# Natural projections 512 columns wide over all token tiles at once, and TensorE's large tiles at multiples of 256 bytes

## The chip, the cores and the metric

The kernel runs on one core of a Trainium2 chip. The metric is the device time of one execution in microseconds; three runs of the kernel before took 2058.98, 2060.18 and 2060.73 us, median 2060.18 us. Five engines work in a core: TensorE (PE in the profile) multiplies, VectorE (DVE), ScalarE (ACT) and GpSimd (POOL) do the rest, and SyncE (SP) issues the DMAs. TensorE accumulates in PSUM, which has eight banks of 512 floats in each of 128 partitions; the other engines read the results there.

## The reference

One layer of a hybrid decoder trunk over a prompt of 2048 tokens and a sample group of 8 x 8 = 64 tokens, model width 1024, all in float32. Cut to what matters here:

```
h = rmsnorm(x) @ w_in                                   # 1024 columns in, all branches out
q, k, v, z_a, gate_b, gate_c, h_b, z_b, u, v_c, z_c, g = split(h)
q = rmsnorm(q per head of 64); k = rmsnorm(k per head)   # q: 512 columns, 8 heads
y_a = window attention(q, k, v)                          # banded, 128 positions, sinks
y_b = gate_b * causal_conv3(gate_c * h_b)
v_c = rmsnorm(v_c)                                       # 512 columns, one norm per token
y_c = u * (tril(w_s[group]) @ v_c + b_s)                 # mixing of the 128 positions of a chunk
m = sum over branches of sigmoid(g_i) * ((silu(z_i) * y_i) @ w_out_i)
y = x + m @ w_o
```

The change touches how q and v_c (the chunk v) are projected and normed, and where tiles lie in memory. What is computed stays the same.

## The kernel before

**Precision.** Every float32 operand of a large product is split (`split`, L167 on ScalarE and L168 on VectorE) into a high part that TensorE takes at full rate and a low rest; each product is three matmuls: high x high, high x low, low x high.

**Two forms of product.** In the *transposed* form (`gemm_t`, L176 to L178) a 128x128 weight block is stationary and the tokens move, 512 columns at a time: `xh`, `xl` (the split normed input), `mh`, `ml` (the merged branches) or `br0h` to `br2l` (the branch outputs). In the *natural* form (`natural`, L285 to L287) 128 tokens are stationary and 256 weight columns move, so that a token's features lie along the free dimension and can be normed there. A natural token tile is 8 blocks of 128 rows x 3 matmuls = 24 matmuls.

**Stages.** The tokens go through in four superblocks of four token tiles; the last also has the 64 sample tokens, and its 576 columns move as two chunks of 288. In each superblock: `kv_phase` (natural), `q_phase` (natural, two passes of 256 columns over all token tiles, each tile evicted from its own `ps_mm` buffer, of which there are three), z_A and the convolution branch (transposed, with attention between them), `chunk_phase` (u and z_C transposed, then v natural), `gate_phase` (per 128 output columns and branch 24 matmuls with `xh`/`xl`, then 12 with `br`), `out_phase` (`m`). The chunk v goes through in two passes: the first puts 256 columns of all four token tiles into the four quarters of the PSUM tile `first`, the second puts the other 256 columns of a tile into a `ps_mm`, after which that tile is evicted.

**Evictions.** Of q: ScalarE squares (L297), VectorE sums per head (L299), POOL forms the inverse root (`rstd`, L163 and L164), VectorE multiplies (L390). Of chunk v: ScalarE squares and sums each half (L688), VectorE adds the halves (L692), POOL (L163, L164), VectorE multiplies each half (L697), `split` into `vbuf`; 2.5 and 3.0 ticks later two `spatial` pieces mix the tile's positions: four matmuls each into a `ps_tp` (two buffers; L674, L675), two additions on VectorE (L677, L678), after the second a multiply (L653) and a split into `br2`.

**What sets the order.** Each engine runs its instructions in the order of the program. Weights arrive as units of 512 KB (256 KB for w_out), loaded by SP and split ahead of use in a fixed list (`order`, `take`). Pieces of other work are put between the matmuls by `later(delay, fn)`; `tick` advances a clock by 0.25 for every six matmuls of 512 columns (every twelve of a natural tile of 256), and runs what is due. Tiles of one `tag` share memory; the framework makes an instruction wait where it would overwrite what another engine has still to read, and it tracks this by PSUM tile.

**Addresses.** Tiles are laid out per partition in the order of their allocation. `consts` comes first, then `xh`, `xl`, `kst`, `vst` and `hist` (32 bytes) in `res`, then the rest. In the program as built, `xh`, `xl`, `kst`, `vst` and `wsp` start 32 bytes above a multiple of 256, and what lies behind `hist` (`mh`, `ml`, `br*`, `rbuf`, `vbuf`, the weights `wh`, `wl`) 64 bytes above one.

Of the kernel before, what the change touches and what calls it, by code (L numbers as in the profile page):

```python
# [20 lines left out]
NTS = NS * TS  # L21
NT = SEQ + NTS
HD = 64
EPS = 1e-6
KT = D // P
# [23 lines left out]
def trunk_kernel(ctx: ExitStack, tc: tile.TileContext, A, O):  # L49
    nc = tc.nc  # L50
# [8 lines left out]
    def ps_mm():  # L59
        return psum.tile([P, 512], F32, tag="mm", name="ps_mm", bufs=3)  # L60
# [93 lines left out]
    xh = res.tile([P, KT, TMAX], F32R, name="xh")  # L154
    xl = res.tile([P, KT, TMAX], F32R, name="xl")
    kst = res.tile([P, 2, 5, P], F32R, name="kst")
    vst = res.tile([P, 5 * 256 + 128], F32R, name="vst")
    hist = res.tile([P, 4, 2], F32, name="hist")
    nc.vector.memset(hist, 0.0)

    def rstd(out, ssq, n, width):

        nc.gpsimd.tensor_scalar(out, ssq, 1.0 / width, EPS, ALU.mult, ALU.add)  # L163
        nc.gpsimd.tensor_tensor(out, out, mhalf[: out.shape[0], :n], ALU.pow)  # L164
# [127 lines left out]
    def nunits(chunk):  # L292
        return [take("wn", 2 * chunk + j) for j in range(2)]

    def head_rstd(src, rows, nh, tag):
        sq = side("sq", [P, nh * HD])
        nc.scalar.activation(sq[:rows], src, AF.Square)  # L297
        s = small.tile([P, nh], F32, tag=tag + "s", name=tag + "s")
        nc.vector.tensor_reduce(s[:rows], sq[:rows].rearrange("p (h d) -> p h d", d=HD), AX.X, ALU.add)  # L299
# [75 lines left out]
    def q_phase(sb, samp):  # L375
        _, ntile, _, sample = SBS[sb]
        qn = res.tile([P, 4 * TMAX], F32, tag="br2l", name="qn")
        abuf = samp["abuf"]
        samp["q"] = [x[:NTS, 2048:2304] for x in (qn, abuf)]
        for g in range(2):  # L380
            w = nunits(1 + g)
            for i in range(ntile + sample):
                rows = NTS if i == ntile else P
                o = natural(ps_mm()[:rows, :256], i, rows, w)
                r = head_rstd(o, rows, 4, "q")
                if i == ntile:
                    dst = samp["q"][g]
                else:
                    dst = qn[:, i * 512 + g * 256: i * 512 + (g + 1) * 256]
                nc.vector.scalar_tensor_tensor(  # L390
                    dst.rearrange("p (h d) -> p h d", d=HD),
                    o.rearrange("p (h d) -> p h d", d=HD),
                    HD ** -0.5,
                    r[:rows].unsqueeze(2).broadcast_to([rows, 4, HD]),
                    ALU.mult,
                    ALU.mult,
                )
        return qn, abuf
# [100 lines left out]
    def sample_attention(samp, sbuf, za, br):  # L499
# [24 lines left out]
        def scores(g):  # L524
            kts = samp["kts"]
            sp = psum.tile([P, 2, 256], F32, tag="S", name="sps", bufs=1)
            gs = slice(g * HD, (g + 1) * HD)
            for n in range(NS):
                nn, j = divmod(n, 4)
                lhs = qts[gs, n * 32:(n + 1) * 32]  # L530
                rs = slice(32 * j, 32 * j + 32)
                nc.tensor.matmul(sp[rs, nn, 0:P], lhs, kc[gs, n * P:(n + 1) * P], start=True, stop=True)
                nc.tensor.matmul(sp[rs, nn, P:w], lhs, kts[gs], start=True, stop=True)
            s = sbuf[:, g * 1024:g * 1024 + 2 * w].rearrange("p (a b) -> p a b", a=2)
            nc.sync.dma_start(s, A["biass"][:, g])
            nc.vector.tensor_tensor(s, sp[:, :, 0:w], s, ALU.add)
            nm = small.tile([P, 2], F32, tag="snm", name="snm")
            nc.vector.tensor_reduce(nm, s, AX.X, ALU.max, negate=True)
            nc.vector.tensor_tensor(nm, nm, nsinks_s[:, g:g + 1].broadcast_to([P, 2]), ALU.min)
            den = small.tile([P, 2], F32, tag="sden", name="sden")  # L540
            for nn in range(2):
                nc.scalar.activation(s[:, nn], s[:, nn], AF.Exp, bias=nm[:, nn:nn + 1], accum_out=den[:, nn:nn + 1])
            es = small.tile([P, 2], F32, tag="ses", name="ses")
# [80 lines left out]
    def chunk_phase(sb, br, samp_args):  # L624
# [17 lines left out]
        if sample:  # L642
            os.append(psum.tile([P, 512], F32, tag="pv", name="sfirst", bufs=1)[:NTS, :256])
        w = nunits(3)
        for i in range(ntile + sample):
            natural(os[i], i, NTS if i == ntile else P, w)
        w = nunits(4)

        def mixed(i, rows, t, gg):

            ts = slice(i * P, i * P + rows)
# [27 lines left out]
            if gg.stop == 4:  # L679
                mixed(i, P, t, slice(0, 4))  # L680

        for i in range(ntile + sample):
            rows = NTS if i == ntile else P
            o2 = [os[i][:rows], natural(ps_mm()[:rows, :256], i, rows, w)]
            ssq = small.tile([P, 2], F32, tag="vssq", name="vssq")
            vn = tmp("vn", [P, 512])
            for j in range(2):
                nc.scalar.activation(  # L688
                    vn[:rows, j * 256:(j + 1) * 256], o2[j], AF.Square, accum_out=ssq[:rows, j:j + 1]
                )  # L690
            s1 = small.tile([P, 1], F32, tag="vs1", name="vs1")
            nc.vector.tensor_tensor(s1[:rows], ssq[:rows, 0:1], ssq[:rows, 1:2], ALU.add)  # L692
            r = small.tile([P, 1], F32, tag="vr", name="vr")
            rstd(r[:rows], s1[:rows], 1, 512)
            for j in range(2):
                js = slice(j * 256, (j + 1) * 256)
                nc.vector.scalar_tensor_tensor(vn[:rows, js], o2[j], r[:rows], vnw[:rows, js], ALU.mult, ALU.mult)  # L697
# [157 lines left out]
def _layout(i):  # L855
# [20 lines left out]
    for d in range(KT):  # L876
        order += [tl["g"][8 * b + d] for b in range(3)]
    a["wt"] = np.stack(order)
    nat = [np.concatenate([c["k"], c["v"]], 1), c["q"][:, :256], c["q"][:, 256:], c["vc"][:, :256], c["vc"][:, 256:]]

    a["wn"] = np.stack([x.reshape(2, 4, P, 256).transpose(0, 2, 1, 3) for x in nat]).reshape(10, P, 1024)
# [74 lines left out]
```

## Time and profile before

| | |
|---|---|
| median of three runs | 2060.18 us |
| the profiled execution, its own time | 2059.51 us |
| its span, first to last instruction | 2057.7 us |
| TensorE busy | 2037.0 us, 99 % |
| VectorE, ScalarE, POOL busy | 51 %, 41 %, 5 % |
| mean granted TensorE clock | 0.997 |
| matmul groups L176 to L178 | 749.7 + 740.4 + 740.5 us for `xh`/`xl`, 112.5 + 112.6 + 112.6 us for `m` |
| natural groups L285 to L287 into `ps_mm` | 156.4 + 154.1 + 154.3 us |

The profile is of one execution; 1.8 us of its time lie outside its span. A group's row has busy time, mean duration of one in ns, and the idle time ahead of them with what ended it. A timeline row has start, duration, engine, line, operation, tile written and tiles read. A matmul's duration holds its pipeline, so neighbours overlap; how fast they follow each other is read from their starts.

### The profile page before, as it was taken

How to read it: one execution, taken by the hardware profiler on the slowest of the kernel's cores; microseconds unless marked ns; L12 is line 12 of the kernel's file. 1: busy time of each engine (PE TensorE's matmuls, PEld its weight loads, DVE VectorE, ACT ScalarE, POOL GpSimd, SP SyncE). 2: the span in 40 equal slices, each digit the busy share in tenths (PEclk: the TensorE clock that was granted, in tenths of full speed). 3: DMA queues.
4: the chain of work that ended last, by engine and by line, in shares of the span. 5: the costliest groups of instructions: out<-in, count | busy, mean ns of one | idle time of the engine just before them, and what ended most of it. 6: DMA issues, size and time to landing. Idle time of an engine off the chain costs nothing.

```text
span 2057.7 us, 29142 instructions
## 1 busy us (share of the span) xinstructions
PE 2037.0 (99%) x11703; PEld 1794.7 (87%) x11703; DVE 1057.5 (51%) x1869; ACT 850.8 (41%) x1513; POOL 96.2 (5%) x168
## 2 busy tenths in 40 slices
PE   6999999999999999999999999999999999999999
PEld 6888888888988898888988888888899999999999
DVE  6586253335588353335478535334557842533332
ACT  5675233332576233333367423333347641422330
POOL 3100000000200000000200000000030000000000
PEclk9999999999999999999999999999999999999999
DMA  6222233336222223335322223333622341222233
GB/s 192 94 82 82 82 102 119 117 108 220 83 77 78 93 74 116 113 95 192 129 93 70 84 72 106 125 105 120 201 87 52 56 129 57 65 83 88 78 103 107
DMA packets 85702, 212.36 MB, mean 103 GB/s; under 512 B 18224, under 2 KB 23344, under 8 KB 85552
## 3 DMA queue, kind: packets, MB, share of 16 engines
q1 hardware_dynamic: 85536, 209.53, 32.7%
q8 instruction: 92, 1.51, 0.3%
q10 hardware_dynamic: 32, 0.98, 0.1%
q14 instruction: 42, 0.34, 0.1%
HBM read 201.46 MB, written 10.00 MB: 103 GB/s over the span
## 4 chain that ended last, share of the span: by engine, by line
PE 98%; ACT 1%; DVE 1%; DMA 0%; POOL 0%; issue 0%; SPq 0%; DVEq 0%
PE ps_mm L176 27%; PE ps_mm L177 27%; PE ps_mm L178 27%; PE ps_mm L287 3%; PE ps_mm L285 3%; PE ps_mm L286 3%; PE ps_tp L468 1%; PE sp L444 1%; PE sp L443 1%; PE first L287 1%; PE first L286 1%; PE first L285 1%; PE pv L475 1%; PE pv L476 1%; PE ps_tp L674 0%; PE ps_tp L675 0%
## 5 line engine op out<-in xcount | busy, mean ns | idle before, releaser
L176 PE MATMUL ps_mm<-xh,wh 128*128 128x512 f32 (+1 forms) x2080 | 749.7, 360 | 0.5 <-ACT za L830 0.5
L178 PE MATMUL ps_mm<-xh,wl 128*128 128x512 f32 (+1 forms) x2080 | 740.5, 356 | 0.0
L177 PE MATMUL ps_mm<-xl,wh 128*128 128x512 f32 (+1 forms) x2080 | 740.4, 356 | 0.0
L168 DVE TENSOR_TENSOR wl<-raw,wh 128x1024 fp32r<-128x1024 f32 x376 | 407.4, 1085 | 528.4 <-ACT wh L167 526.2
L167 ACT CAST wh<-raw 128x1024 fp32r<-128x1024 f32 x376 | 353.0, 940 | 722.4 <-PE ps_mm L177 554.6
L178 PEld LDWEIGHTS ps_mm<-xh,wl 128*128 128x128 f32 x2080 | 392.6, 189 | 56.2
L176 PEld LDWEIGHTS ps_mm<-xh,wh 128*128 128x128 f32 x2080 | 392.6, 189 | 52.5 <-ACT za L830 0.7
L177 PEld LDWEIGHTS ps_mm<-xl,wh 128*128 128x128 f32 x2080 | 393.2, 189 | 51.1
L285 PE MATMUL ps_mm<-wh,xh 128*128 128x256 f32 (+1 forms) x544 | 156.4, 287 | 5.0 <-ACT xh L167 5.0
L286 PE MATMUL ps_mm<-wl,xh 128*128 128x256 f32 (+1 forms) x544 | 154.1, 283 | 1.3 <-DVE wl L168 1.3
L287 PE MATMUL ps_mm<-wh,xl 128*128 128x256 f32 (+1 forms) x544 | 154.3, 284 | 0.9 <-DVE xl L168 0.9
L177 PE MATMUL ps_mm<-ml,wh 128*128 128x512 f32 (+1 forms) x320 | 112.6, 352 | 0.3 <-DVE ml L168 0.3
L178 PE MATMUL ps_mm<-mh,wl 128*128 128x512 f32 (+1 forms) x320 | 112.6, 352 | 0.0
L176 PE MATMUL ps_mm<-mh,wh 128*128 128x512 f32 (+1 forms) x320 | 112.5, 351 | 0.0
L742 DVE TENSOR_TENSOR t<-ps_mm,t 128x512 f32<-128x512 f32 (+1 forms) x120 | 71.5, 596 | 76.6 <-PE ps_mm L178 75.2
L285 PEld LDWEIGHTS ps_mm<-wh,xh 128*128 128x128 f32 (+1 forms) x544 | 102.8, 189 | 6.5 <-ACT xh L167 6.3
L286 PEld LDWEIGHTS ps_mm<-wl,xh 128*128 128x128 f32 (+1 forms) x544 | 102.7, 189 | 1.8 <-DVE wl L168 1.6
L287 PEld LDWEIGHTS ps_mm<-wh,xl 128*128 128x128 f32 (+1 forms) x544 | 102.6, 189 | 1.4 <-DVE xl L168 1.3
L726 ACT ACTIVATE t<-ps_mm,c_bg 128x512 f32<-128x512 f32 (+1 forms) x120 | 73.0, 609 | 72.4 <-PE ps_mm L178 72.3
L431 ACT ACTIVATE rbuf<-ps_tp,c_qnw 64x256 fp32r<-64x256 f32 x128 | 60.0, 469 | 23.8 <-PE ps_tp L423 12.4
L177 PEld LDWEIGHTS ps_mm<-ml,wh 128*128 128x128 f32 x320 | 60.1, 188 | 7.9 <-DVE ml L168 0.6
L176 PEld LDWEIGHTS ps_mm<-mh,wh 128*128 128x128 f32 x320 | 60.1, 188 | 7.5
(203 smaller groups left out, 2565.2 us busy)
## 6 DMA issues: line engine op xcount, KB each, us to landing
raw<-in_wt SPq DMA_DIRECT2D x208, 512.0 KB
raw<-in_wout SPq DMA_DIRECT2D x96, 256.0 KB
raw<-in_wn SPq DMA_DIRECT2D x40, 512.0 KB
raw<-in_wo SPq DMA_DIRECT2D x32, 512.0 KB
xbuf<-in_xn SPq DMA_DIRECT2D x12, 512.0 KB
xt<-in_xt SPq DMA_DIRECT2D x24, 256.0 KB
out_yt<-xt SPq DMA_DIRECT2D x24, 256.0 KB
xbuf<-in_xt SPq DMA_DIRECT2D x16, 256.0 KB
```

What stands on the lines that cost most here:

```text
L167: nc.scalar.copy(hi, src)
L168: nc.vector.tensor_tensor(lo, src, hi.bitcast(F32), ALU.subtract)
L176: nc.tensor.matmul(o, wh[:, ws], rh(k, c0, c1), start=k == 0, stop=False)
L177: nc.tensor.matmul(o, wh[:, ws], rl(k, c0, c1), start=False, stop=False)
L178: nc.tensor.matmul(o, wl[:, ws], rh(k, c0, c1), start=False, stop=k == kts - 1)
L285: nc.tensor.matmul(o, xh[:, k, ts], wh[:, ws], start=k == 0, stop=False)
L286: nc.tensor.matmul(o, xh[:, k, ts], wl[:, ws], start=False, stop=False)
L287: nc.tensor.matmul(o, xl[:, k, ts], wh[:, ws], start=False, stop=k == KT - 1)
L431: nc.scalar.activation(hh[half, :, e], src, AF.Copy, scale=qnw2[es])
L443: nc.tensor.matmul(sp[:, h, k0:], b["hh"][:, hs], rhs, start=True, stop=False)
L726: nc.scalar.activation(t[:, c0:c1], pg[:, : c1 - c0], AF.Sigmoid, bias=bg[:, 8 * b + d:8 * b + d + 1])
L742: nc.vector.tensor_tensor(t[:, c0:c1], pa[:, : c1 - c0], t[:, c0:c1], ALU.mult)
```

## The change

Two edits.

1. `q_phase` and the chunk v use `wide`: the outer loop runs over four weight units of 2 blocks x 512 columns (the layout of the units in memory is changed for it), the inner one over the token tiles, six matmuls of 512 columns each. All accumulators of 512 columns are open at once: token tiles 0 and 1 in the halves of one PSUM tile `wide`, tile 2 in `widep`, tile 3 (and the sample) in `ps_mm`. A tile is evicted as soon as its six matmuls of the last unit are issued: q with one square, one sum over eight heads, one inverse root of eight, two multiplies; chunk v with one square, one inverse root, one multiply.
2. `hist` moves to `consts` and an unused tile of 192 bytes follows it. In the program as built, `xh`, `xl`, `kst`, `vst`, `wsp`, `mh`, `ml`, `br*`, `rbuf`, `vbuf`, `wh` and `wl` all start at a multiple of 256 bytes. Three small sample tiles (`snm`, `sden`, `ses`) get two buffers instead of four.

```diff
-    hist = res.tile([P, 4, 2], F32, name="hist")
+    hist = consts.tile([P, 4, 2], F32, name="hist")
+
+    consts.tile([P, 48], F32, name="pad")
...
+    def wide_outs(n, sample):
+
+        s4 = psum.tile([P, 4, 256], F32, tag="S", name="wide", bufs=1)
+        outs = [s4[:, 0:2].rearrange("p a b -> p (a b)"), s4[:, 2:4].rearrange("p a b -> p (a b)")]
+        outs.append(psum.tile([P, 512], F32, tag="pv", name="widep", bufs=1)[:, :])
+        outs += [ps_mm()[:, :] for _ in range(n + sample - 3)]
+        return [(o[:NTS] if i == n else o[:, :], NTS if i == n else P) for i, o in enumerate(outs)]
+
+    def wide(j0, outs):
+
+        for u in range(4):
+            wh, wl = take("wn", j0 + u)
+            for i, (o, rows) in enumerate(outs):
+                ts = slice(i * P, i * P + rows)
+                for kk in range(2):
+                    k = 2 * u + kk
+                    ws = slice(kk * 512, (kk + 1) * 512)
+                    nc.tensor.matmul(o, xh[:, k, ts], wh[:, ws], start=k == 0, stop=False)
+                    nc.tensor.matmul(o, xh[:, k, ts], wl[:, ws], start=False, stop=False)
+                    nc.tensor.matmul(o, xl[:, k, ts], wh[:, ws], start=False, stop=k == KT - 1)
+                tick(0.25)
+                if u == 3:
+                    yield i, o, rows
...
-        for g in range(2):
-            w = nunits(1 + g)
-            for i in range(ntile + sample):
-                rows = NTS if i == ntile else P
-                o = natural(ps_mm()[:rows, :256], i, rows, w)
-                r = head_rstd(o, rows, 4, "q")
...
+        for i, o, rows in wide(2, wide_outs(ntile, sample)):
+            r = head_rstd(o, rows, 8, "q")
+            for g in range(2):
+                gs = slice(g * 256, (g + 1) * 256)
+                dst = samp["q"][g] if i == ntile else qn[:, i * 512 + g * 256: i * 512 + (g + 1) * 256]
                 nc.vector.scalar_tensor_tensor(
                     dst.rearrange("p (h d) -> p h d", d=HD),
-                    o.rearrange("p (h d) -> p h d", d=HD),
+                    o[:, gs].rearrange("p (h d) -> p h d", d=HD),
                     HD ** -0.5,
-                    r[:rows].unsqueeze(2).broadcast_to([rows, 4, HD]),
+                    r[:rows, 4 * g:4 * g + 4].unsqueeze(2).broadcast_to([rows, 4, HD]),
...
-        first = psum.tile([P, 4, 256], F32, tag="S", name="first", bufs=1)
-        os = [first[:, i] for i in range(ntile)]
...
-        w = nunits(3)
-        for i in range(ntile + sample):
-            natural(os[i], i, NTS if i == ntile else P, w)
-        w = nunits(4)
...
-        for i in range(ntile + sample):
-            rows = NTS if i == ntile else P
-            o2 = [os[i][:rows], natural(ps_mm()[:rows, :256], i, rows, w)]
...
+        for i, o, rows in wide(6, wide_outs(ntile, sample)):
+            ssq = small.tile([P, 1], F32, tag="vssq", name="vssq")
             vn = tmp("vn", [P, 512])
...
+            nc.scalar.activation(vn[:rows], o, AF.Square, accum_out=ssq[:rows])
             r = small.tile([P, 1], F32, tag="vr", name="vr")
-            rstd(r[:rows], s1[:rows], 1, 512)
...
+            rstd(r[:rows], ssq[:rows], 1, 512)
+            nc.vector.scalar_tensor_tensor(vn[:rows], o, r[:rows], vnw[:rows], ALU.mult, ALU.mult)
```

The units keep their size, number and place in SP's list. On TensorE, 1632 natural matmuls of 256 columns become 816 of 512.

The first place is TensorE at the end of the first superblock's q. Before, the border between two token tiles of the second pass (a tile's last matmuls, then the next tile's first into another buffer):

```order
L285 MATMUL ps_mm<-wh,xh 128x256
L286 MATMUL ps_mm<-wl,xh 128x256
L287 MATMUL ps_mm<-wh,xl 128x256
L285 MATMUL ps_mm<-wh,xh 128x256 [waits DVE_49,Activation_49]
L286 MATMUL ps_mm<-wl,xh 128x256
```

After, the same place in the last unit: the end of tile 3's six matmuls of the unit before, tile 0's six, and the start of tile 1's:

```order
L316 MATMUL ps_mm<-wh,xl 128x512
L314 MATMUL wide<-wh,xh 128x512 [waits Activation_49]
L315 MATMUL wide<-wl,xh 128x512 [waits DVE_49]
L316 MATMUL wide<-wh,xl 128x512
L314 MATMUL wide<-wh,xh 128x512
L315 MATMUL wide<-wl,xh 128x512
L316 MATMUL wide<-wh,xl 128x512
L314 MATMUL wide<-wh,xh 128x512 [waits DVE_49,Activation_49]
L315 MATMUL wide<-wl,xh 128x512
```

Before, the wait on VectorE and ScalarE is for the reads of the tile that held this `ps_mm` buffer three tiles ago. After, the wait of tile 1's first matmul is for the reads of tile 0, whose six matmuls stand just ahead of it; tile 0's own two waits are for the split weights of the unit.

The second place is VectorE's queue there. Before, the last two evictions of q, of 256 columns each:

```order
L168 TENSOR_TENSOR wsp<-wsr,wsp 128x4x128 [waits Activation_49]
L299 TENSOR_REDUCE qs<-sq 128x4 [waits Activation_49]
L390 SCALAR_TENSOR_TENSOR qn<-ps_mm,qr 128x256 [waits Pool_49]
L168 TENSOR_TENSOR wl<-raw,wh 128x1024 [waits DMAHW3_49,Activation_49]
L299 TENSOR_REDUCE qs<-sq 128x4 [waits Activation_49]
L168 TENSOR_TENSOR wl<-raw,wh 128x1024 [waits DMAHW4_49,PE_49,Activation_49]
L390 SCALAR_TENSOR_TENSOR qn<-ps_mm,qr 128x256 [waits Pool_49]
```

After, all of tile 0's and tile 1's:

```order
L325 TENSOR_REDUCE qs<-sq 128x8 [waits Activation_49]
L170 TENSOR_TENSOR wsp<-wsr,wsp 128x4x128 [waits Activation_49]
L411 SCALAR_TENSOR_TENSOR qn<-wide,qr 128x256 [waits Pool_49]
L411 SCALAR_TENSOR_TENSOR qn<-wide,qr 128x256
L325 TENSOR_REDUCE qs<-sq 128x8 [waits Activation_49]
L411 SCALAR_TENSOR_TENSOR qn<-wide,qr 128x256 [waits Pool_49]
```

A tile's sum, its wait for POOL and its two multiplies now follow each other, and tile 1's sum stands behind tile 0's multiplies; `wsp` (split once, in the first superblock) stands inside.

The third place is TensorE at the start of `gate_phase` in the first superblock, where the spatial pieces come due. Before, two of them, then twelve `br0` matmuls, of which the first two are shown, ahead of the next four:

```order
L674 MATMUL ps_tp<-wsp,vbuf 128x256
L675 MATMUL ps_tp<-wsp,vbuf 128x256
L674 MATMUL ps_tp<-wsp,vbuf 128x256
L675 MATMUL ps_tp<-wsp,vbuf 128x256
L176 MATMUL ps_mm<-br0h,wh 128x512
L177 MATMUL ps_mm<-br0l,wh 128x512
```

After, between two such groups stand six:

```order
L686 MATMUL ps_tp<-wsp,vbuf 128x256
L687 MATMUL ps_tp<-wsp,vbuf 128x256
L178 MATMUL ps_mm<-xh,wh 128x512
L179 MATMUL ps_mm<-xl,wh 128x512
L180 MATMUL ps_mm<-xh,wl 128x512
L178 MATMUL ps_mm<-xh,wh 128x512
L179 MATMUL ps_mm<-xl,wh 128x512
L180 MATMUL ps_mm<-xh,wl 128x512
L686 MATMUL ps_tp<-wsp,vbuf 128x256
L687 MATMUL ps_tp<-wsp,vbuf 128x256
```

The groups of spatial matmuls stand six matmuls apart where they stood twelve apart.

More of the change, by code (lines that the diff above doesn't have):

```diff
@@ L639, in chunk_phase @@
         vbuf = res.tile([P, 4 * 1024], F32R, tag="mh", name="vbuf")
-        first = psum.tile([P, 4, 256], F32, tag="S", name="first", bufs=1)
-        os = [first[:, i] for i in range(ntile)]
-        if sample:
-            os.append(psum.tile([P, 512], F32, tag="pv", name="sfirst", bufs=1)[:NTS, :256])
-        w = nunits(3)
-        for i in range(ntile + sample):
-            natural(os[i], i, NTS if i == ntile else P, w)
-        w = nunits(4)
         def mixed(i, rows, t, gg):
@@ L878, in _layout @@
     a["wt"] = np.stack(order)
-    nat = [np.concatenate([c["k"], c["v"]], 1), c["q"][:, :256], c["q"][:, 256:], c["vc"][:, :256], c["vc"][:, 256:]]
-    a["wn"] = np.stack([x.reshape(2, 4, P, 256).transpose(0, 2, 1, 3) for x in nat]).reshape(10, P, 1024)
+    kv = np.concatenate([c["k"], c["v"]], 1).reshape(2, 4, P, 256)
+    a["wn"] = np.concatenate(
+        [kv.transpose(0, 2, 1, 3).reshape(2, P, 1024)]
+        + [x.reshape(4, 2, P, 512).transpose(0, 2, 1, 3).reshape(4, P, 1024) for x in (c["q"], c["vc"])]
+    )
     wa = np.asarray(i["w_out_a"])[0][perm]
```

20 lines of the change are left out of this document (3 added, 17 removed).

## The prediction

> **What bounds the kernel now.** I read the page first, then the waits of TensorE, then its time table, in that order: does TensorE ever stop, and how fast do its matmuls follow each other when it does not.
>
> ```profile
> span 2057.7 us, 29142 instructions
> PE 2037.0 (99%) x11703; PEld 1794.7 (87%) x11703; DVE 1057.5 (51%) x1869; ACT 850.8 (41%) x1513; POOL 96.2 (5%) x168
> PE 98%; ACT 1%; DVE 1%; DMA 0%; POOL 0%; issue 0%; SPq 0%; DVEq 0%
> PE ps_tp L266 <- POOL xr L164: 8.8, 3, 6.5
> PE ps_mm L285 <- ACT xh L167: 5.0, 4, 4.0
> ...
> PE ps_tp L674 <- DVE sp L678: 0.2, 1, 0.2
> ```
>
> TensorE is busy 99 % of the span, 98 % of the chain that ended last is its own, and its waits add up to under 20 us, nearly all before the first superblock's stream is running. So the time is the number of matmuls times their pitch (start to start), and two things can change it: the pitch, or a new stop. A matmul's listed duration holds its pipeline; the pitch comes from stretches without a gap (start, duration, PE busy, matmuls, granted clock, DMA share, GB/s; the count takes in one that reaches in from before):
>
> ```profile
> core 0: us, PE busy (x), PEclk, DMA share, GB/s
> 188.07:237.07 49.00, 49.00 (x211) 1.00 0.29 92
> 237.07:259.47 22.40, 22.40 (x193) 1.00 0.17 59
> 464.12:507.65 43.53, 43.53 (x193) 1.00 0.69 230
> 1656.37:1674.53 18.16, 18.16 (x138) 1.00 0.38 88
> 2015.90:2041.34 25.44, 25.44 (x194) 1.00 0.36 114
> ```
>
> The first row is z_C/u tiles with `xh`, `xl` moving, 512 columns: 49.00/210 = 233.3 ns. The second is the natural projection of v, 256 columns: 22.40/192 = 116.7 ns. The third is `mh`, `ml`, 512 columns: 43.53/192 = 226.7 ns, at a DMA share twice as high, so traffic is not what makes the first row slow. The last two are 288 columns, `xh`/`xl` 18.16/137 = 132.6, `mh`/`ml` 25.44/192 = 132.5. The program's addresses differ in one respect: `xh`, `xl` start 32 bytes above a multiple of 256, the `m`, `br` and weight tiles 64 bytes above one. The groups by shape say the same in modelled durations:
>
> ```profile
> L177 PE MATMUL ps_mm<-xl,wh 128*128 128x512 f32 x1248 | 493.9, 396 | 0.0
> L177 PE MATMUL ps_mm<-ml,wh 128*128 128x512 f32 x192 | 74.8, 389 | 0.0
> L177 PE MATMUL ps_mm<-br1l,wh 128*128 128x512 f32 x96 | 37.7, 392 | 0.0
> ```
>
> **The gain.** After the change all of these start at a multiple of 256, a start that no row shows. I take for it the best pitch that is shown, 226.7, and keep two bounds: no gain, and the removal of all that does not grow with columns. For the second: from 288 to 512 columns the pitch grows by (226.7 - 132.5)/224 = 0.42 ns a column, 215.3 ns for 512.
> - 512-column `xh`/`xl`: 3 x 1248 = 3744 matmuls x 6.6 = 24.7 us.
> - `br`: 9 groups of 96 = 864, whose groups stand 2 to 3 ns above `m` because they follow `xh`: 864 x 2 = 1.7 us.
> - q and chunk v: 17 token tiles x 24 x 2 products = 816 matmuls of 512 columns take the place of 1632 of 256. At the old start this is nothing, 2 x 116.7 = 233.4 against 233.3; at 226.7 it is 816 x 6.7 = 5.5 us.
> - 288 columns, kv (still 256) and attention: nothing, since the two 288 rows agree within 0.1 ns; the bound is in the first rival.
>
> Sum: **-32 us**. The Trainium skill (TensorE: Matmul & The Clock Gate, "Back-to-back issue gap") states N/2.4 GHz plus about 2.5 ns between warm matmuls, 215.8 ns for 512 columns. No row here is that fast; by it 512-column matmuls lose another 10.9 ns each.
>
> **The new stop.** Before, a token tile's 24 matmuls were finished one tile after another, each into its own `ps_mm` (or a quarter of `first`, which was full before anything read it). Now all four finish in the last weight unit, six matmuls apart, and token tiles 0 and 1 are halves of one PSUM tile, `wide`. As the order shows, tile 1's first matmul of that unit waits for the engines that evict tile 0; TensorE issues in order, so tiles 2 and 3 queue behind it. This happens for q and for chunk v in each of four superblocks. What one stop lasts is tile 0's eviction, which the timeline of a q tile prices today, off the path:
>
> ```profile
> 539.26 0.28 PE L287 MATMUL ps_mm<-wh,xl 128*128 128x256 f32 x1
> 539.58 0.39 ACT L297 ACTIVATE sq<-ps_mm 128x256 f32<-128x256 f32 x1 [2.42 <-PE ps_mm L287]
> 539.99 0.42 DVE L299 TENSOR_REDUCE qs<-sq 128x4 f32<-128x256 f32 x1 [0.31 <-ACT sq L297]
> 540.50 0.19 POOL L163 TENSOR_SCALAR qr<-qs 128x4 f32<-128x4 f32 x1 [1.28 <-DVE qs L299]
> 540.78 1.01 POOL L164 TENSOR_TENSOR qr<-qr,mhalf 128x4 f32<-128x4 f32 x1
> L164 POOL TENSOR_TENSOR qr<-qr,mhalf x34: 999/1006/1012, 42.4 to 1525.7; 128x4 f32<-128x4 f32 x32, 64x4 f32<-64x4 f32 x2
> L164 POOL TENSOR_TENSOR kr<-kr,mhalf x17: 688/696/703, 21.3 to 1497.3; 128x2 f32<-128x2 f32 x16, 64x2 f32<-64x2 f32 x1
> L479 ACT COPY abuf<-pv 64x512 f32<-64x512 f32 x32 | 18.5, 578 | 17.3 <-PE pv L476 17.0
> L390 DVE SCALAR_TENSOR_TENSOR qn<-ps_mm,qr 128x256 f32<-128x256 f32 x32 | 13.6, 425 | 40.3 <-POOL qr L164 40.3
> ```
>
> Last matmul to square 0.32, +0.11 for 512 columns: 0.43. Square to reduce 0.41, with a 512-column ScalarE read of PSUM (0.58 for 0.39): 0.60. Reduce to POOL 0.51; 512 elements instead of 256 lengthen it by an estimated 0.25: 0.76. POOL's first 0.28. Its power from 1.01 for four elements and 0.70 for two, 0.155 an element, to eight: 1.62. Two multiplies 0.42 each, and 0.1 of hand-overs. Sum 4.6, less the 0.23 pitch that passes anyway: 4.4 us, x4 = **17.6**. Chunk v has one element in its power:
>
> ```profile
> 251.28 0.38 ACT L688 ACTIVATE vn<-ps_mm 128x256 f32<-128x256 f32 x1 [1.80 <-PE ps_mm L287]
> 251.56 0.20 ACT L688 ACTIVATION_READ_ACCUMULATOR vn<-ps_mm 128x1 f32 x1
> 252.03 0.19 POOL L163 TENSOR_SCALAR vr<-vs 128x1 f32<-128x1 f32 x1 [186.62 <-DVE vs L692]
> 252.31 0.56 POOL L164 TENSOR_TENSOR vr<-vr,mhalf 128x1 f32<-128x1 f32 x1
> L603 DVE SCALAR_TENSOR_TENSOR t<-cin,c_cw,t 128x512 f32<-128x512 f32 x32 | 23.7, 742 | 0.1
> ```
>
> 0.43 to the square, 0.47 to its accumulator read (0.28 here, +0.19), 0.3 to POOL now that the addition between is gone, 0.28, 0.59, one 512-column multiply 0.74, less 0.23: 2.7 us, x4 = **10.8**. The other evictions follow behind work: the matmuls of two more tiles and of the next `t_tiles`. The second square, the second reduce and POOL pair and the addition that fall away were hidden by matmuls and give nothing.
>
> **The clock after a stop.** The granted clock falls to half near the start:
>
> ```profile
> 22.68:26.10 3.42, 2.75 (x19) 1.00 0.73 167
> 26.10:29.51 3.41, 2.21 (x13) 1.00 0.09 23
> 29.51:32.92 3.41, 3.36 (x17) 0.50 0.03 7
> ```
>
> Thirteen matmuls in 3.41 us (pitch shares: some 40 % of full stream) were followed by a window at half clock, nineteen (over 50 %) were not. Half clock costs 3.41 x (1 - 16 x 0.1167/3.41) = 1.5 us a window. A 4.4 us stop takes at least 2.2 us, 64 %, out of one such window wherever it falls: 1.6 each, 6.4. A 2.7 us one takes 2.0 in about two cases of three: 1.0 to 1.1 each, 4.4. Together **11**, bounds 0 and 13 (eight windows). The Trainium skill (the same page, "What's actually happening") lets the clock fall after a fully idle window of about 3.4 us; by that a 4.4 us stop would do it in (4.4 - 3.4)/3.4, three cases of ten, and this term would be 2. The half clock above followed a window with thirteen matmuls in it, so I go by the row.
>
> **Spatial pieces.** `later` places the position mixing by ticks after each chunk-v tile. When tiles ended a whole tick-step apart, its eight pieces per superblock were spread over two ticks, 48 matmuls or 11.2 us; now they lie within 1.25 ticks, 7 us.
>
> ```profile
> L677 DVE TENSOR_TENSOR sp<-ps_tp,c_bsb 128x256 f32<-128x256 f32 x32 | 12.8, 417 | 3.0 <-PE ps_tp L675 2.9
> L653 DVE TENSOR_TENSOR sp<-sp,suc 128x512 f32<-128x512 f32 x16 | 10.9, 682 | 0.0
> L168 DVE TENSOR_TENSOR br2l<-sp,br2h 128x512 fp32r<-128x512 f32 x16 | 11.0, 689 | 2.6 <-ACT br2h L167 2.1
> ```
>
> VectorE owes 8 x 2 x 0.417 + 4 x (0.682 + 0.689) = 12.2 us for them, and weight splits besides; TensorE may run two `ps_tp` buffers ahead. I take 2 us of waiting per superblock, **8**, bounds 0 and 12 (three each). In the last superblock the sample is a fifth tile, `ps_mm`'s three buffers hold tile 3, the sample and one tile of the next product, and TensorE must wait once for the serial evictions: **4**, bounds 0 and 8.
>
> **Sum.** -32 + 17.6 + 10.8 + 11 + 8 + 4 = +19 on the profiled execution's 2059.5 (1.8 more than its span, for what lies outside it; 0.7 under the median of the runs): 2079, and on the median **2080**. With both ends of the last three terms 2057 to 2090; stops a quarter longer would add 7: 2097. About 0.2 %, 4 us, is what a measurement of this kernel can tell from no change. SP's loads keep their order and size, and DMA is not waited for.
>
> **Rivals.**
> 1. *A start at 256 removes the whole excess* (faster). 512 columns go to 215.3: a further 11.4 x (3744 + 864 + 576 + 816 = 6000) = 68; the 288-column ones, 2496 + 576 + 384 = 3456, lose the same 11.2 each, 39; kv 408 x 9 = 4. So 111 less, **1970**; half of it 2025. It beats the stops once the 512 pitch falls below about 224.6. For it: the start does matter between 32 and 64, and all operands move at once, weights included. Against: between 288 and 512 columns the `m` pitch already grows at one column per 0.42 ns, so what is left looks like a cost per matmul, and the 288 rows do not see the start at all.
> 2. *The start is not the cause* (slower still). Then nothing is gained and the stops stay: 2059.5 + 51 = **2111**. A start at 32 and at 64 would be alike, and the 233.3 due to the operand's region or its neighbours in time; but `br` groups, which stand between `xh` groups, show 392 against 396. The Trainium skill (SBUF — State Buffer, "Specifications (TRN2)") counts in lines of 16 bytes, of which 32, 64 and 256 are all multiples; the rows 396 and 389 speak against it.
> 3. *The stop does not bite*: halves are told apart, or evictions are over in time. -32 + 8 + 4 = **2040**. The wait stands in the instruction, so little speaks for it.
>
> **Chances.** The forecast 0.53, the first rival 0.35 (0.33 of it more than 4 us faster), the second 0.08, the third 0.04. Of the forecast's own 0.53, 0.02 falls to faster and 0.05 within 4 us. Faster 0.33 + 0.04 + 0.02 = 0.39; same 0.07; slower 0.54. Cases of both signs hold the chance, so the range reaches from 1985, the middle of the first rival's better half, to 2100, leaving about 0.12 below and 0.06 above; the forecast's own range is 2057 to 2097.
>
> **What would show it.** In the waits of TensorE: eight stops on `wide`, near 4.4 and 2.7 us, released by VectorE's multiplies, and PEclk of 0.50 in windows after them. In the stretch without gaps: 512-column `xh` at 226.7 (forecast), 215 (first rival) or 233 (second). In the groups: `ps_tp` waiting for `sp`, some microseconds. The forecast is wrong if `xh` at 512 goes below 224, or if TensorE's waits stay under 20 us.

## The result and the profile after

The changed kernel takes 2092.47 us, median (2090.77 to 2092.88), beside 2060.45 for the kernel before: ratio 1.0155, 95 % interval 1.0137 to 1.0172. It is slower, by 32 us where 20 were forecast. The profiled execution's span grew from 2057.7 to 2089.0 us. The page after, on the lines that answer to those shown of before:

```profile
span 2089.0 us, 27338 instructions
PE 2026.9 (97%) x10887; PEld 1763.5 (84%) x10887; DVE 1052.3 (50%) x1818; ACT 847.6 (41%) x1462; POOL 82.6 (4%) x134
PE 93%; DVE 2%; ACT 2%; issue 1%; POOL 1%; DMA 0%; SPq 0%; ACTq 0%; DVEq 0%; POOLq 0%
```

TensorE is busy 10 us less and the span is 31 us longer: its work got cheaper, and it now stands. The chain of waits, 98 % TensorE before, has 5 % of VectorE, ScalarE and POOL in it. The waits of TensorE name where (in us: total, times, longest):

```profile
PE wide L314 <- DVE qn L411: 18.3, 4, 4.6
PE wide L314 <- DVE vn L700: 10.1, 4, 2.5
PE ps_tp L686 <- DVE sp L690: 9.4, 4, 2.8
...
PE ps_mm L178 <- DVE qn L411: 2.8, 1, 2.8
...
PE ps_tp L672 <- issue: 1.2, 1, 1.2
```

The first two rows are the eight stops of tile 1 on tile 0's eviction, forecast at 17.6 and 10.8; the third is the spatial pieces (8), the fourth the last superblock's `ps_mm` (4). On the other side the pitch. A stretch of u/z_C tiles without a gap, and the groups by shape:

```profile
191.33:238.70 47.37, 47.37 (x210) 1.00 0.32 95
L179 PE MATMUL ps_mm<-xl,wh 128*128 128x512 f32 x1248 | 486.6, 390 | 0.0
L179 PE MATMUL ps_mm<-ml,wh 128*128 128x512 f32 x192 | 74.7, 389 | 0.0
```

In that row 47.37 us from the start of the first of 210 matmuls to the start of the last are 209 pitches of 226.7 ns, where 233.3 stood before. `xh`/`xl` now run like `m`, which itself has not moved. 226.7 is also the floor: the first rival's 215 does not appear.

If the time from each matmul's start to the next one's is summed by group, the change of the span is made up so: 512-column `xh`/`xl` -21.1; `br` +1.4 (its pitch gained 1.5, half clock took the rest); the natural matmuls with their stops +33.7; the spatial ones +12.0; 288-column `xh`/`xl` with the `ps_mm` wait +4.2; the rest +1. Together +31.

One stop, the q of the second superblock (start, duration, engine; the idle time before it in brackets):

```profile
542.00 0.60 ACT L323 ACTIVATE sq<-wide 128x512 f32<-128x512 f32 x1 [0.26 <-PE wide L316]
542.92 0.68 DVE L325 TENSOR_REDUCE qs<-sq 128x8 f32<-128x512 f32 x1
543.68 0.20 POOL L165 TENSOR_SCALAR qr<-qs 128x8 f32<-128x8 f32 x1 [16.38 <-DVE qs L325]
543.97 1.64 POOL L166 TENSOR_TENSOR qr<-qr,mhalf 128x8 f32<-128x8 f32 x1
545.63 0.76 DVE L411 SCALAR_TENSOR_TENSOR qn<-wide,qr 128x256 f32<-128x256 f32 x2 [2.04 <-POOL qr L166]
546.53 0.76 PE L314 MATMUL wide<-wh,xh 128*128 128x512 f32 x1 [4.57 <-DVE qn L411]
```

This is the chain of the prediction step by step; the power of eight elements takes 1.64 us (1.62 estimated), the stop 4.57.

### The profile page after: what moved, and what is told of

It is laid out like the page before. It is cut to its first block, busy times and chain, and to the rows that moved or that the text cites. A ratio compares the mean times of both kernels' runs of the same rounds, so it can differ in the third digit from the quotient of the medians.

```text
span 2089.0 us, 27338 instructions
## 1 busy us (share of the span) xinstructions
PE 2026.9 (97%) x10887; PEld 1763.5 (84%) x10887; DVE 1052.3 (50%) x1818; ACT 847.6 (41%) x1462; POOL 82.6 (4%) x134
## 4 chain that ended last, share of the span: by engine, by line
PE 93%; DVE 2%; ACT 2%; issue 1%; POOL 1%; DMA 0%; SPq 0%; ACTq 0%; DVEq 0%; POOLq 0%
PE ps_mm L178 26%; PE ps_mm L180 25%; PE ps_mm L179 25%; PE wide L314 1%; PE wide L315 1%; PE wide L316 1%; PE ps_tp L489 1%; PE ps_mm L314 1%; PE ps_mm L316 1%; PE ps_mm L315 1%; POOL qr L166 1%; PE sp L465 1%; PE widep L314 1%; PE widep L315 1%; PE sp L464 1%
## 5 line engine op out<-in xcount | busy, mean ns | idle before, releaser
L178 PE MATMUL ps_mm<-xh,wh 128*128 128x512 f32 (+1 forms) x2080 | 741.7, 357 | 3.3 <-DVE qn L411 2.8
L179 PE MATMUL ps_mm<-xl,wh 128*128 128x512 f32 (+1 forms) x2080 | 732.8, 352 | 0.0
L314 PE MATMUL wide<-wh,xh 128*128 128x512 f32 x128 | 53.4, 417 | 28.4 <-DVE qn L411 18.3
L180 PEld LDWEIGHTS ps_mm<-mh,wl 128*128 128x128 f32 x320 | 60.1, 188 | 7.5
L475 ACT ACTIVATE sbuf<-sbuf,nm 128x256 f32<-128x256 f32 (+1 forms) x128 | 62.8, 492 | 3.7 <-DVE nm L472 3.2
L768 DVE TENSOR_TENSOR xt<-ps_mm,xt 128x512 f32<-128x512 f32 (+1 forms) x40 | 23.9, 597 | 75.2 <-PE ps_mm L180 45.5
L178 PE MATMUL ps_mm<-br1h,wh 128*128 128x512 f32 (+1 forms) x160 | 57.6, 360 | 0.0
L179 PE MATMUL ps_mm<-br1l,wh 128*128 128x512 f32 (+1 forms) x160 | 57.4, 359 | 0.0
```

What stands on the lines that cost most here:

```text
L178: nc.tensor.matmul(o, wh[:, ws], rh(k, c0, c1), start=k == 0, stop=False)
L179: nc.tensor.matmul(o, wh[:, ws], rl(k, c0, c1), start=False, stop=False)
L180: nc.tensor.matmul(o, wl[:, ws], rh(k, c0, c1), start=False, stop=k == kts - 1)
L314: nc.tensor.matmul(o, xh[:, k, ts], wh[:, ws], start=k == 0, stop=False)
L475: nc.scalar.activation(s[:, h, k0:], s[:, h, k0:], AF.Exp, bias=nm[:, h:h + 1], accum_out=den[:, h:h + 1])
```

## The experiments

### The second edit alone

```diff
 (kernel before)
-    hist = res.tile([P, 4, 2], F32, name="hist")
+    hist = consts.tile([P, 4, 2], F32, name="hist")
+    consts.tile([P, 48], F32, name="pad")
```

> The kernel before with the second edit alone (all large tiles of TensorE start at a multiple of 256 bytes); q and the chunk v go through in two passes of 256 columns as before. Theory (the start sets the pitch): 512-column xh at 226.7 ns, no stops; -24 for xh/xl, -1.5 for br, and, since the 256-column kv matmuls of the changed kernel showed 119 to 120 ns instead of 117, +5 for the 2040 matmuls of 256 columns: about 2040 us. Rival (the faster pitch came with the wide form or the new weight layout, not with the start): xh at 233, 2060 us.

2041.56 us, ratio 0.991 (0.9893 to 0.9926). The theory holds: `xh`/`xl` -21.2, `br` -1.5 us, no new wait. Not foreseen in the prediction, but visible in the changed kernel's kv: 256-column matmuls got slower. The group of chunk v's first pass, before and here:

```profile
L287 PE MATMUL first<-wh,xl 128*128 128x256 f32 x128 | 35.8, 280 | 0.0
```

```profile
L289 PE MATMUL first<-wh,xl 128*128 128x256 f32 x128 | 36.2, 283 | 0.0
```

Start to start it is 119.9 ns for 116.7; over all 2040 natural matmuls +5.0 us.

### The first edit alone

```diff
 (changed kernel)
-    hist = consts.tile([P, 4, 2], F32, name="hist")
-    consts.tile([P, 48], F32, name="pad")
+    hist = res.tile([P, 4, 2], F32, name="hist")
```

> The changed kernel with the second edit undone: hist back behind vst, no pad, so xh and xl start 32 bytes and the weights 64 bytes above a multiple of 256. Theory: all stops and half-clock windows stay, the pitch of xh goes back to 233 and the wide matmuls (weights moving, start at 64) stay near 227: 2092.5 + 21 to 26 = about 2116 us. Rival (pitch comes with the wide form): 2092 us.

2116.16 us, ratio 1.0274 (1.0253 to 1.0295). The four runs reach from 2112 to 2123 us. The stops stay (18.9 and 10.1 us), and `xh` is back at 233. But the wide matmuls, for which I had expected 227, went to 234 (median from start to start, 227 in the changed kernel). One of their groups, in the changed kernel and here (the durations also hold the half-clock stretches):

```profile
L316 PE MATMUL wide<-wh,xl 128*128 128x512 f32 x128 | 51.8, 405 | 0.0
```

```profile
L314 PE MATMUL wide<-wh,xl 128*128 128x512 f32 x128 | 53.6, 419 | 0.0
```

Their moving operand, the weights, starts 64 bytes above a multiple of 256, as `mh` and `ml` do, which run at 226.7. The prediction had put 233 for wide matmuls at the old start without giving a reason; if the start of the moving operand decided, as I read it here, they would belong with `m`. This was the first sign that this reading was wrong.

### Separate PSUM tiles

```diff
 (changed kernel)
-        s4 = psum.tile([P, 4, 256], F32, tag="S", name="wide", bufs=1)
-        outs = [s4[:, 0:2]..., s4[:, 2:4]...]
-        outs.append(psum.tile([P, 512], F32, tag="pv", name="widep", bufs=1)[:, :])
-        outs += [ps_mm()[:, :] for _ in range(n + sample - 3)]
+        outs = [ps_mm()[:, :] for _ in range(2)]
+        s4 = psum.tile([P, 4, 256], F32, tag="S", name="wide", bufs=1)
+        outs.append(s4[:, 0:2]...)
+        outs.append(psum.tile([P, 512], F32, tag="pv", name="widep", bufs=1)[:, :])
+        outs += [ps_mm()[:, :] for _ in range(sample)]
```

> The changed kernel with other PSUM tiles: token tiles 0 and 1 in two ps_mm buffers, tile 2 in half of the tile of two banks, tile 3 in widep, the sample in the third ps_mm. No two token tiles share a PSUM tile. Theory: the eight stops of 18.3 + 10.1 us, the 2.8 us at the next ps_mm, and with them about 18 us of half clock go; the ps_tp waits of 9.4 us stay: 2092.5 - 49 = about 2043 us, mean clock back at 0.997. Rival (the wide form itself makes the clock fall or the evictions late, whatever tile they are in): waits of 10 to 20 us turn up at the next ps_mm or sp, half-clock windows stay, 2060 to 2075 us.

2061.71 us, ratio 1.0007 (0.9998 to 1.0017): 31 us better than the changed kernel, 18 short of what I expected. The eight stops are gone, so they were due to the shared tile. But the rival has a part in it:

```profile
PE ps_tp L687 <- DVE sp L691: 9.4, 4, 2.8
...
PE ps_mm L178 <- DVE abuf L412: 3.3, 1, 3.3
PE sp L466 <- DVE rbuf L454: 2.6, 4, 1.1
PE sp L465 <- ACT rbuf L453: 1.7, 3, 0.6
```

All four evictions of q come due within 4 us and run one after another on VectorE and POOL; without the stop, attention's first pieces (`rbuf`, from q) reach TensorE before they are ready, and each such wait was followed by a half-clock stretch (at 69.9, 554.5 and 1039.2 us). Half clock still cost about 11.6 us here, where it cost about 14 in the changed kernel (below). My 18 us for it were the count of windows times 1.6 and did not allow for the part of a half-clock window in which TensorE stands anyway.

### Separate tiles, and the spatial pieces two ticks apart

```diff
 (the run before)
-                    later(AT_SPATIAL + SPATIAL_EVERY * j, ...)
+                    later(AT_SPATIAL - 0.5 + 0.25 * i + SPATIAL_EVERY * j, ...)
```

> As the run with separate PSUM tiles, and the spatial pieces lie two ticks apart again: a piece of token tile i is due at 2.0 + 0.25 i (+ 0.5) ticks after its tile instead of 2.5 (+ 0.5). Theory: the ps_tp waits of 9.4 us fall to under 2: about 8 us less than the run with separate tiles alone, about 2035 us. Rival (VectorE owes the same work either way and br2 is only later): the wait moves to the br2 matmuls, the same time as without the spreading.

2047.7 us, ratio 0.9941 (0.9926 to 0.9955). The waits of `ps_tp` on `sp` are gone, and only 0.5 us appear at `br2l`: 14 us less, where 8 were expected. Of these, 9.4 are waits, and the rest are the half-clock windows that had followed them (at 762.8 and 1247.5 us in the run before, 1.5 each) and fewer others.

### Is 64 enough?

```diff
 (kernel before)
-    hist = res.tile([P, 4, 2], F32, name="hist")
+    hist = consts.tile([P, 4, 2], F32, name="hist")
```

> The kernel before with hist moved and no pad: every large tile of TensorE starts 64 bytes above a multiple of 256; nothing else changes. Theory (a multiple of 64 is enough, 256 adds nothing): 512-column xh at 226.7 ns as with the start at 256, -21 and -1.5 us, and the natural matmuls of 256 columns keep 116.7 ns, which the start at 256 had made 119: 2060 - 22.5 = about 2037 us, 5 less than the run with the start at 256 alone. Rival (the distance to 256 counts by steps): xh between 227 and 233, 2045 to 2055 us.

2040.9 us, ratio 0.9906 (0.9891 to 0.992), the same as with the start at 256, in both parts: `xh` 226.8 ns, and 119.9 ns for 256 columns, not the 116.7 that I expected:

```profile
L177 PE MATMUL ps_mm<-xl,wh 128*128 128x512 f32 x1248 | 486.5, 390 | 0.0
L286 PE MATMUL first<-wl,xh 128*128 128x256 f32 x128 | 36.2, 283 | 0.0
```

No start at a multiple of 256 is needed for the gain. What 64 and 256 have in common is that `xh`, `xl` and the weights now start at the same place modulo 256.

### xh at a multiple of 256, the weights, m and br 32 above

```diff
 (kernel before)
+    hist = consts.tile([P, 4, 2], F32, name="hist")
+    consts.tile([P, 48], F32, name="pad")
 (behind vst)
+    res.tile([P, 8], F32, name="pad2")
```

> The kernel before with xh, xl, kst, vst, wsp at a multiple of 256 and all that lies behind them (m, br, rbuf, vbuf, the weights wh and wl) 32 bytes above one. Theory (the start of the moving operand counts): xh at 512 columns 227 ns although its stationary weights lie at 32; m and br at 512 columns 233; 2060 - 21 + 1440 x 6.5 ns = 9, about 2048 us, with the 256-column natural ones (weights moving) somewhere between. Rival (the start of the stationary operand counts, or of both): xh stays at 233, 2060 to 2070 us.

2060.88 us, one run: the whole gain is gone. The first row is `xh`, `xl` moving, the second `mh`, `ml`, as in the prediction's table:

```profile
188.24:237.01 48.77, 48.77 (x211) 1.00 0.30 92
464.30:507.59 43.29, 43.29 (x192) 1.00 0.69 230
```

`xh` at a multiple of 256 follows at 48.77/209 = 233.3 ns; `m`, 32 bytes off a multiple of 64, at 43.29/191 = 226.7. So where the moving operand starts does not decide, and neither does the start of the stationary weights, which is 32 for both rows. What is left is the place of one against the other: equal in every fast case so far, apart in every slow one.

### A distance of 64

```diff
 (kernel before)
-    hist = res.tile([P, 4, 2], F32, name="hist")
+    hist = res.tile([P, 16], F32, name="hist")[:, 0:8].rearrange("p (a b) -> p a b", a=4)
```

> The kernel before with hist widened from 32 to 64 bytes in its old place: xh and xl start 32 bytes above a multiple of 256 as before, the weights, m and br 96 bytes above one. Nothing of TensorE's lies at a multiple of 64, but moving and stationary start a multiple of 64 apart, where before it was 32. Theory (formed on the run with xh at 0 and the weights at 32: the distance between the two operands counts, not where each lies): xh at 512 columns 227 ns, the 256-column natural ones 120 instead of 117, about 2041 us. Rival (a start at a multiple of 64 is needed for both operands): xh at 234, 2060 us or more.

2060.57 us, ratio 1.0001 (0.9992 to 1.001):

```profile
188.27:237.03 48.76, 48.76 (x211) 1.00 0.29 92
464.30:507.60 43.30, 43.30 (x193) 1.00 0.69 231
```

`xh` stays at 233.3, `m` (at 96, as the weights) at 226.7. A distance that is a multiple of 64 is not enough; my theory of the moment was too wide, and the rival (both at a multiple of 64) has `m` against it.

### Many distances in one run

```diff
 (kernel before)
+    res.tile([P, 16], F32, name="padx")      # behind xh
+    res.tile([P, 8], F32, name="padk")       # behind hist
+    res.tile([P, 8], F32, name="padm")       # between mh and ml
+    res.tile([P, 8 or 16], F32, ...)         # before br0h and before br0l
```

> The kernel before with small unused tiles between the large ones, so that one run holds many distances between the start of the moving operand and that of the weights (which lie at 32 modulo 256; modulo 256 the distance of xh is 0, xl 64, mh 128, ml 160, br0h 192, br0l, br1h, br1l 0, br2h and br2l 160). Theory (the distance modulo 256, or 128, decides and not where each operand lies): at 512 columns 227 ns for xh, br0l and br1, 233 for xl, ml, br0h and br2; mh at 128 tells 128 from 256; 3744 xh/xl matmuls of which two thirds are faster, about 2045 to 2055 us. Rival (both operands must start at a multiple of 64 or 256): everything at 233, 2060 to 2070 us.

2058.57 us, ratio 0.9991 (0.9981 to 1.0):

```profile
L179 PE MATMUL ps_mm<-xl,wh 128*128 128x512 f32 x1248 | 491.3, 394 | 0.0
L178 PE MATMUL ps_mm<-br0h,wh 128*128 128x512 f32 x96 | 38.1, 397 | 0.0
L179 PE MATMUL ps_mm<-br0l,wh 128*128 128x512 f32 x96 | 38.0, 396 | 0.0
L179 PE MATMUL ps_mm<-br1l,wh 128*128 128x512 f32 x96 | 37.4, 390 | 0.0
```

`br1h`, `br1l`, all at 32 like the weights, run at 226.7 ns from the third of a tile's twelve matmuls on (the first two, behind `xh` and `xl`, take 233 and 231): no multiple of 64 is needed, and the rival falls. But `br0l`, at distance 0 too, takes 237 ns in the median beside `br0h` at 192, and `xh` at distance 0 takes 231 beside `xl` at 64. So it isn't each pair by itself: the three matmuls of a product run fast together when high part, low part and weights all start at the same place modulo 256, which is the case in every fast 512-column group of all runs and in no slow one. That is why the run won about 2 us, with an interval that reaches 1.0, and not the 6 to 16 I had put. `mh` at 128 with `ml` at 160 lay between, 229.0 ns on average; whether a common distance of 128 is free, so that 128 and not 256 is the number that counts, was not tried.

### A longer stop

```diff
 (changed kernel, in head_rstd)
+        if nh == 8:
+            nc.gpsimd.tensor_tensor(sq[:rows, :nh], s[:rows], mhalf[:rows, :nh], ALU.pow)
```

> The changed kernel with one more POOL instruction in q's eviction (a power of eight elements whose result is not used), 1.6 to 1.7 us. Theory (a stop lasts as long as tile 0's eviction): the stops on wide for q grow from 4.6 to 6.2 us each, 18.3 to 25 in all; with 0 to 2 more half-clock windows and attention's first pieces a little later: 2099 to 2106 us. Rival (POOL's part is hidden behind the other tiles' matmuls): 2092 us.

2129.03 us, ratio 1.0327 (1.0309 to 1.0345). The stop behaves as expected, 25.1 us in four instead of 18.3:

```profile
PE wide L314 <- DVE qn L413: 25.1, 4, 6.3
PE sp L467 <- DVE rbuf L455: 13.4, 3, 4.6
...
PE ps_mm L178 <- DVE qn L413: 8.1, 1, 8.1
```

But the whole costs 37 us, not 7 to 14: every tile's eviction is 1.7 us longer, the four run in series, so attention's first scores wait 13 us more and the last superblock's `ps_mm` 5.3 more, each with half clock behind it. In the changed kernel this series ended just about when its users came; there was next to no slack behind the first stop.

### A stop filled with matmuls that nobody needs

```diff
 (changed kernel, in wide, after tile 0's eviction in the last unit)
+                    if i == 0:
+                        fill = ps_tp()
+                        for _ in range(16 if j0 == 2 else 8):
+                            nc.tensor.matmul(fill[:, :], xh[:, 0, 0:P], wh[:, 0:512], start=True, stop=True)
```

> The changed kernel with matmuls that nobody needs inside the stops: after tile 0's six matmuls of the last unit 16 (q) or 8 (chunk v) of 512 columns into a ps_tp that is not read. Theory (the clock falls because TensorE stands still, and costs 1.6 us a window): the stop stays as long, 3.6 or 1.8 us of it are now matmuls, and the seven half-clock windows after q and three after chunk v go: 2092.5 - 16 = about 2076 us, though TensorE does 96 matmuls more. Rival (the clock falls with something else around the stop, or costs little): 2090 to 2095 us.

2085.73 us, ratio 1.0124 (1.0107 to 1.0141). With 96 matmuls more the kernel is 7 us faster. The waits on `wide` shrink to 3.8 and 2.9 us, the difference being matmuls, and the half clock after q's stops is gone. The waits, the q stop of the second superblock, and the span and mean granted clock here and in the changed kernel:

```profile
PE wide L314 <- DVE qn L415: 3.8, 4, 0.9
PE wide L314 <- DVE vn L704: 2.9, 4, 0.7
...
543.58 3.79 PE L323 MATMUL ps_tp<-wh,xh 128*128 128x512 f32 x16
548.31 0.47 PE L314 MATMUL wide<-wh,xh 128*128 128x512 f32 x1 [0.94 <-DVE qn L415]
...
core 0: 2084.4 us, clock 0.995
core 0: 2089.0 us, clock 0.988
```

So the clock after q's stops falls because TensorE stands. It is 7 us and not 16: what the changed kernel lost in the windows after q is 7.4 us (next part), and after chunk v there was nothing to win.

### The wide form without its waits

```diff
 (separate tiles, spread pieces; q_phase)
+        last = None
         for i, o, rows in wide(2, wide_outs(ntile, sample)):
             r = head_rstd(o, rows, 8, "q")
-            ... multiplies of tile i
+            if last:
+                scaled(*last)          # multiplies of the tile before
+            last = (i, o, rows, r)
+        scaled(*last)
...
-        sbuf = attention(sb, qn, abuf, za, br, 0.0, UNIT_EVERY)
+        sbuf = attention(sb, qn, abuf, za, br, 0.5, UNIT_EVERY)
```

> The run with separate tiles and spread pieces, and two more edits in the order: in q the multiplies of a token tile are issued after the square and sum of the next one, so that VectorE doesn't wait for POOL in between, and attention starts half a tick later. Theory: the waits of 2.6 + 1.7 us at sp and 3.3 us at ps_mm behind the sample's eviction go, and with them two or three half-clock windows: 2047.7 - 8 - 4 = about 2036 us, less than the second edit alone. Rival (the wide form bunches the evictions and they only wait elsewhere): 2044 to 2048 us.

2039.36 us, ratio 0.9898 (0.9881 to 0.9914). The waits at `sp` are gone; the one at `ps_mm` behind the sample's eviction is not, it grew to 4.7 us. One more edit puts the sample first of the five tiles:

```diff
-        outs = [ps_mm()[:, :] for _ in range(2)]
+        outs = [(i, ps_mm()[:, :]) for i in ([n] if sample else []) + [0, 1]]
```

> The run with separate tiles, spread pieces, the multiplies of q one tile later and attention half a tick later, and one more edit: in the last superblock the sample comes first of the five tiles, so that its eviction is first in the chain and its ps_mm is free when z_A wants it. Theory: the 4.7 us at ps_mm and the two half-clock windows after them go: 2039.4 - 8 = about 2031 us. Rival (z_A then waits for tile 0 or 1 instead): 2036 to 2039 us.

2034.09 us, ratio 0.9875 (0.986 to 0.989): 26 us faster than the kernel before, 58 than the changed one, 7 than the second edit alone (the two intervals, 0.986 to 0.989 and 0.9893 to 0.9926, do not touch). The two longest waits of TensorE are those of the start again; the third is in the last superblock's q, at 1473.5 us, where the sample now comes first:

```profile
PE ps_tp L268 <- POOL xr L166: 9.0, 3, 6.8
PE ps_mm L287 <- ACT xh L169: 5.1, 5, 3.7
PE ps_mm L314 <- ACT abuf L388: 1.8, 1, 1.8
```

## Why the prediction was right, and where it was not

**The sign and the stop.** Right, by its own steps. The shared PSUM tile holds TensorE eight times, for 18.3 and 10.1 us against 17.6 and 10.8. (The terms put for chunk v add up to 2.6 us and not to the 2.7 that was taken; four times 2.6 is 10.3.) Separate tiles took these waits away, and a longer eviction made q's longer.

**The gain.** 32 us were put, about 27 came: `xh`/`xl` 21.1 instead of 24.7, because the pitch of all 3744 fell by 5.7 ns on average where an unbroken stretch gains 6.6 (in the changed kernel too, the second to the ninth matmul behind a group of attention's take 228 to 232 ns, and only from the eleventh on 226.7); `br` 1.5; the wide matmuls about what was put (in the last run, free of stops, all natural ones take 246.9 us start to start beside 252.3); and the step "288 columns, kv and attention: nothing" left out that 256-column matmuls lose 3 ns, 1 us here, 5 where q and v stay narrow. The pitch of 226.7 was chosen rightly, its reason was not: the start of `xh` above a multiple of 256 is not what decides, as the runs with other starts show. The number held by luck, because the edit that moved `xh` to a multiple of 256 also brought it to the same place as the weights. Before, the program had `xh` and the weights 32 apart and `m` and the weights at the same place, and I read off the first number of each pair and not the distance.

**The clock.** 11 us were put and about 11 came (matmuls in half-clock windows, pitch less full pitch: about 14 us, about 3 before), but not where I put them, so that the sums agree is luck. The windows around a q stop, around a chunk-v stop and around a stop at the spatial pieces:

```profile
541.43:544.85 3.42, 0.54 (x3) 1.00 0.26 46
544.85:548.26 3.41, 1.73 (x4) 0.50 0.27 108
548.26:551.67 3.41, 3.41 (x9) 0.50 0.00 0
...
254.72:258.13 3.41, 2.05 (x10) 1.00 0.00 0
258.13:261.55 3.42, 2.26 (x10) 1.00 0.28 77
261.55:264.96 3.41, 3.41 (x17) 1.00 0.00 0
...
278.61:282.02 3.41, 1.11 (x7) 1.00 0.00 0
282.02:285.43 3.41, 2.94 (x9) 0.50 0.26 77
```

After a q stop two windows run at half clock in three superblocks, one in the first: 7.4 us for 6.4. After chunk v there were none in four, where I had put two falls in three: its 2.5 us fell across two windows, and the emptier one was still busy for 60, 60, 48 and 53 % in the four superblocks. That is chance as well: in the run with the first edit alone and in the one with the longer stop, half clock followed the same 2.5 us in two superblocks of four each. The spatial stops of 2.8 us, to which I had given no clock at all, emptied a window to a third and cost a window each in three superblocks, about 4 us; the `ps_mm` wait cost 1.5. So the rule by which I priced it (a window with some 40 % or less is followed by half clock, counted in matmuls times pitch) agrees with these. Over all runs, behind the first 15 us and apart from the sample's small matmuls, every full-clock window with less than a third of a full stream was followed by half clock and none with more than 46 %; in between, both happened. The fully idle window of the Trainium skill (TensorE: Matmul & The Clock Gate, "What's actually happening") fits the q stop of the first superblock, where the window 53.32:56.74 held no matmul. It does not fit the falls shown here: the windows before them still had 0.54 and 1.11 us of matmuls in them.

**Spatial pieces and the last superblock.** The waits were 9.4 us where 8 were put and 2.8 where 4 were put, both inside their bounds.

**Not priced.** Some 5 us of small things: the restart after each of the eight stops (start to start they take 29.7 us more than a pitch, 1.3 more than their idle time), attention's first scores in the first superblock 1.4, the sample's attention 1.3, its spatial piece 1.2. With the 5 us of gain that did not come and 1.4 at the spatial pieces these are nearly all of the 12 us between 2080 and 2092.

**The rivals.** The first (215 ns) falls: in no run do 48 of the 512-column matmuls in a row go below 226.7 on average. So the 215.8 that the Trainium skill gives for the isolated warm gap (TensorE: Matmul & The Clock Gate, "Back-to-back issue gap") is not reached by these matmuls. The second (the start is no cause) falls with the second edit alone. The third falls with the eight waits.

## What to carry to other kernels

When accumulators that finish one after another share a PSUM tile, and the framework tracks reads by tile as here, the first eviction stops the next tile's matmuls; give each its own tile, and let the first ones finished be those whose buffers are wanted first. An edit that makes many tiles finish together bunches their evictions and all that is timed behind them, so the delays and the order that were tuned for the old spacing have to be set again: here that was worth 28 us, beside 31 for the separate tiles. And where one half of a change gains and the other loses, time the halves apart before judging either.

## What the runs showed of the hardware that was not expected

The pitch of these 512-column matmuls depends on how the operands lie to each other. It is 226.7 ns when the high part, the low part and the weights start at the same place modulo 256 (0, 32, 64 and 96 were seen). When they do not, it is 232 to 234 on the average of a product's three matmuls (distances of 32, 64, 160 and 192 were seen, single matmuls among them taking from 227 to 237), with 229 for a mixture of 128 and 160. The slow pitch also carries over: in the kernel before, the first five of the twelve `br` matmuls, which stand behind `xh` and `xl`, take 231.3 ns on average, the other seven 226.6, although `br` and the weights start at the same place.

At 288 columns there is no difference (132.5 ns). At 256 columns it is the other way round: 119.9 ns at the same place, 116.7 at a distance of 32 and 117.8 at 64. With the sample's 64 tokens as the stationary operand, 256 columns follow the rule of 512 again: 113.8 ns at the same place, 117 to 119 at distances of 32 and 64. Why was not found out; the runs show the rule, not the mechanism.
